# A macaron encoder layer on one Trainium2 core: other pacing of the normalised chunks, norm vectors split once, squares in two buffer tags, half of the last norm's mean added on TensorE

## The chip, the cores and the metric

The kernel runs on one core of one Trainium2 chip. The metric is the device time of one execution in microseconds (us); the number compared is the median of several runs. Engines are named as in the profile: PE is TensorE (matmuls), PEld its weight loads, DVE is VectorE, ACT is ScalarE, POOL is GpSimd, and SP is the queue from which most DMAs are issued.

## The reference

One encoder layer of width 2048 on 256 tokens with 16 learned meta tokens put in front (272 columns in all):

```python
h = LN(ALPHA*h + 0.5*SwiGLU_1(h))                 # norm n1
u = h @ W_in                                      # latents, mLSTM input, output gate
y = [RMSNorm(MLA(u_mla)) | mLSTM_bidir(u_mlstm)] @ W_out
h = LN(ALPHA*h + y)                               # norm n2
h = LN(ALPHA*h + 0.5*SwiGLU_2(h))                 # norm n3
return h[:, 16:]                                  # meta tokens dropped
# SwiGLU(x) = (silu(x @ w_gate) * (x @ w_up)) @ w_down, hidden width 5632
# LN(x) = (x - mean) * rsqrt(var + 1e-5) * g + b
```

All arrays are float32.

## The kernel before

Activations lie transposed, as 16 chunks `z[0..15]` of 128 features by 272 (later 256) tokens; two chunks share one tile `zs[i]`. Every matrix product is made in split precision: a float32 operand is written as a rounded part (hi) and the rest (lo), and `mm3` (L219) sums hi·hi, hi·lo and lo·hi. `mm2` (L225) makes the first two in one matmul of 512 columns.

**Weights.** All weights stream through one line of units of 128 x 1024 (class `Weights`, L78). `_next` (L118) is called when PE's program reaches a new unit. It loads up to four units ahead and splits two units ahead (`_ahead`, L98): ACT casts hi (L113), DVE subtracts to get lo (L114). hi and lo have three buffers each, so a split can start only when PE has left the unit three before. After that `_next` pops at most one entry of `later`, a list of side work that is thus spread at one entry per unit. The whole plan uses 624 units; the constant `UNITS` is 640, so near the end up to four unused units are loaded and two split.

**The order on the engines.** The kernel's program is a straight list. A planner orders each engine's queue from it ahead of time: among the instructions that it reckons ready, the one that stands earliest in the program goes first, so side work that is ready early can move ahead. Once built, each queue is fixed and runs in order.

**Norms.** `Norm` (L263) gathers a layer norm while its chunks are produced. Once chunk number `at` is there, `shift` (L292) subtracts an estimate of the mean; from then on each chunk goes through `sums` (L308): ACT squares it (L305, tile tag `sq`, two buffers), POOL adds chunk and square to running sums (L318, L319), and `scale` (L322) makes chunk times gain in split form for the early product described next. In `scale` ACT multiplies (L328), POOL copies two columns of the gain and bias vectors to the end of the tile (L330), ACT casts (L216) and DVE subtracts (L217).

**The reader of a norm.** `norm_into` (L424) starts the next product before the norm is known: four PSUM tiles (`qt` after n1, `ft` after n2) are made from chunk times gain, and the mean and the scale are put in afterwards by `settle` (L401). At its chunk 4, `rows` (L379) makes the row vectors, and the 16 normalised chunks (`chunk`, L388) become due: ACT makes the bias row (L392), DVE multiplies and adds (L393, L394), ACT casts (L396), POOL subtracts (L398). They are queued on `later` in eight entries (1, 3, ..., 15), and each entry makes two chunks. The next product reads them: four tiles `xm` of 272 columns after n1 (L580), four tiles of feed-forward 2 after n2 (`ffn_up`, L456). Either uses one unit of weights for two chunks, eight units in all. Between the early product and this reader stand the four `settle` steps of the query latents (L543) or the two bodies of `late` (L1048, each two `settle`, a SiLU on ACT, a product and a split).

**The tail.** After the last matmul of feed-forward 2, `moments` (L359) makes the sums of n3. The variance goes through POOL's power (L376), and PE spreads the result over the partitions (`spread`, L249, L258). Meanwhile DVE adds the mean row to all eight pairs `zs` (L1074). Then DVE multiplies each pair by the spread scale (L1078), ACT (six pairs) or POOL (two) apply gain and bias (L1084, L1082), and SP sends each pair out (L1085).

Of the kernel before, what the change touches and what calls it, by code (L numbers as in the profile page):

```python
# [10 lines left out]
F32 = mybir.dt.float32  # L11
F32R = mybir.dt.float32r
AF = mybir.ActivationFunctionType
ALU = mybir.AluOpType
AX = mybir.AxisListType

P = 128
DM = 2048
SEQ = 256
NM = 16  # L20
L = SEQ + NM
# [10 lines left out]
NCD = DM // P  # L32
# [5 lines left out]
ROPE_BASE = 10000.0  # L38
SCALE = (128 + ROPE) ** -0.5
UNIT = 1024  # L40
UNITS = 640
NQ = 4
O_KV = QL
O_KR = QL + KVL
# [33 lines left out]
class Weights:  # L78
# [19 lines left out]
    def _ahead(self):  # L98
        nc = self.nc
        while self.loaded < min(UNITS, self.unit + self.LOADS + 1):  # L100
            u = self.loaded
# [56 lines left out]
def layer(ctx: ExitStack, tc: tile.TileContext, wsrc, xsrc, vsrc, bsrc, csrc, out):  # L158
    nc = tc.nc
    cp = ctx.enter_context(tc.tile_pool(name="cp", bufs=1))  # L160
# [29 lines left out]
    vec = cp.tile([P, NVEC], F32, tag="vec", name="vec")  # L190
    ident = cp.tile([P, P], F32, tag="ident", name="ident")
# [57 lines left out]
    def spread(nm, r, n):  # L249


        def product():
            pr = psum(f"{nm}pr")
            for j, b in enumerate(token_blocks(n)):
                if b % P:
                    nc.tensor.matmul(pr[:, SEQ:L], r[:, j : j + 1].to_broadcast([P, P]), ident[:, P - NM :], start=True, stop=True)
                else:
                    nc.tensor.transpose(pr[:, b : b + P], r[:, j : j + 1].to_broadcast([P, P]), ident)  # L258
            return pr

        return product

    class Norm:  # L263
# [37 lines left out]
                ws.later.append(lambda i=i: (nc.vector.tensor_tensor(self.z[i], self.z[i], cb, ALU.subtract), self.sums(i)))  # L301

        def square(self, c):
            q = sp.tile([P, L], F32, tag="sq", name=f"{self.nm}q{c}")[:, : self.n]
            nc.scalar.activation(q, self.z[c], AF.Square)  # L305
            return q

# [14 lines left out]
        def scale(self, c):  # L322

            g = col(f"{self.ln}_g", c)
            if not self.early:
                return
            s = scratch(f"{self.nm}e{c}")
            nc.scalar.mul(s[:, :SEQ], self.z[c][:, :SEQ], g)  # L328
            o = VEC[f"{self.ln}_g"][0] + 2 * c
            nc.gpsimd.tensor_copy(s[:, SEQ : SEQ + 2], vec[:, o : o + 2])  # L330
            self.e[c] = big(f"{self.nm}e{c}p")
            split(self.e[c], s[:, : SEQ + 2])

        def last(self):
            self.q = self.square(NCD - 1)
# [43 lines left out]
        def rows(self):  # L379

            nm, n = self.nm, self.n
            pr = self.product()
            self.r = sp.tile([P, L], F32, tag="s1", name=f"{nm}r", bufs=1)[:, :n]
            self.nmr = sp.tile([P, L], F32, tag="s2", name=f"{nm}nmr", bufs=1)[:, :n]
            nc.scalar.copy(self.r, pr[:, :n])
            nc.vector.tensor_tensor(self.nmr, self.mb, pr[:, :n], ALU.mult)
# [37 lines left out]
    def norm_into(norm, tiles):  # L424

        norm.last()
        ws.drain()
        xs = Chunks(norm.chunk)
        at = {
            1: norm.moments,  # L430
            2: lambda: norm.scale(NCD - 1),
            4: lambda: (norm.rows(), [ws.later.append(lambda k=k: xs[k]) for k in range(1, NCD, 2)]),
        }
        outer(tiles, Chunks(lambda k: norm.e[k]), SEQ + 2, at)
        return xs
# [17 lines left out]

        return [(psum(f"{nm}{w[0]}{f}"), f"{nm}_w_{w}", [(f * P, P)]) for f in fs for w in ("gate", "up")]

    def ffn_up(nm, x, n, f0, first, hid):  # L456
        f = f0
        while f < NFT:
            fs = list(range(f, f + (first if f == f0 else 1)))
            f = fs[-1] + 1  # L460
            tiles = ffn_tiles(nm, fs)
            wide = n == SEQ
            if len(fs) > 1:
                outer(tiles, x, n, wide=wide)
            else:
                for t in tiles:
                    outer([t], x, n, wide=wide)
            for j, i in enumerate(fs):
                hid.append(hidden(nm, i, n, tiles[2 * j][0], tiles[2 * j + 1][0], wide))
        return hid  # L470
# [14 lines left out]
    x = Chunks(first)  # L485
    norm = Norm("n1", "ln1", L, z, 2.0 * ALPHA, 4.0 * LN_EPS, True)
    hid = ffn_up("ffn1", x, L, 0, 3, [])
    x = None
    ffn_down("ffn1", hid, L, norm)
    hid = None  # L490
# [4 lines left out]
    x = norm_into(nmx, qt)  # L495
    xt = [(psum(f"xm{i}"), "w_in", [(O_XM + i * P, P)]) for i in range(8)]

    class Latent:
# [19 lines left out]
            self.product = rsqrt(self.nm, self.sum, self.n, self.width)  # L518

        def finish(self):  # L520
            pr = self.product()
            for i in range(self.nt):
                u = self.u[i]
                nc.vector.scalar_tensor_tensor(u, u, col(self.gain, i), pr[:, : self.n], ALU.mult, ALU.mult)
                t = big(f"{self.nm}n{i}")
                split(t, u)
                self.out.append(t)
# [12 lines left out]

    uq = Latent("q", 4, SEQ, "mla_q_norm_g", QL)
    ukv = Latent("kv", 2, L, "mla_kv_norm_g", KVL)
    for i in range(4):  # L543
        t, b = nmx.settle(i, qt[i][0])
        nc.scalar.activation(uq.u[i], t, AF.Identity, bias=b)
        uq.add(i)
# [30 lines left out]
        split(t, s)  # L577
        xc.append(t)

    outer(xt[:4], x, L)  # L580
    for i in range(4):
        conv_in(i)
        ws.later.append(lambda i=i: conv_taps(i))
# [35 lines left out]
    for i in range(2):  # L619
        ps = psum(f"ukv{i}")  # L620
# [3 lines left out]
    ps = psum("kr")  # L624
# [56 lines left out]
    e = cp.tile([P, 3, 2, 4], F32, tag="se", name="se")  # L681
# [206 lines left out]
    x = None  # L888
# [102 lines left out]
    norm = Norm("n2", "ln2", SEQ, z, ALPHA, LN_EPS, True, 6)  # L991
# [10 lines left out]
        norm.product = rsqrt("ao", osum[:, :SEQ], SEQ, DA)  # L1002

    def scale_ya():
        pr = norm.product()
        for h in range(NH):
            o = os_[h // 2][:, h % 2, :SEQ]
            nc.vector.scalar_tensor_tensor(o, o, col("attn_out_g", h), pr[:, :SEQ], ALU.mult, ALU.mult)
            ya[h] = big(f"ya{h}")
            split(ya[h], o)  # L1010
# [20 lines left out]
    p, m = pairs[0], ms[0]  # L1031
    for step in (p.keys, p.values, p.rope_rows, p.queries, m.project_q, m.project_k, m.project_v, p.rotate, p.rope_parts, m.scores):
        step()
    for r in range(XH):
        s = steps(r)
# [11 lines left out]
    x = norm_into(nmx, ft)  # L1047
    hid = []  # L1048

    def late(i):  # L1050
        g, gb = nmx.settle(2 * i, ft[2 * i][0])
        u, ub = nmx.settle(2 * i + 1, ft[2 * i + 1][0])
        nc.scalar.activation(g, g, AF.Silu, bias=gb)
        nc.vector.scalar_tensor_tensor(g, u, ub, g, ALU.add, ALU.mult)
        h = big(f"ffn2h{i}")
        split(h, g)
        hid.append(h)

    for i in range(2):
        late(i)  # L1060
    norm = Norm("n3", "ln3", SEQ, z, 2.0 * ALPHA, 4.0 * LN_EPS, False)
    hid = ffn_up("ffn2", x, SEQ, 2, 2, hid)
    x = None
    ffn_down("ffn2", hid, SEQ, norm)
    norm.last()
# [3 lines left out]
    def both(t):  # L1069
        return t[:, :SEQ].unsqueeze(1).to_broadcast(twice)  # L1070

    with tc.issue_after(norm.var.ins):
        for t in zs:
            nc.vector.tensor_tensor(t[:, :, :SEQ], t[:, :, :SEQ], both(norm.mb), ALU.add)  # L1074
    pr = norm.product()
    for i, t in enumerate(zs):
        o = big(f"o{i}", F32)
        nc.vector.tensor_tensor(t[:, :, :SEQ], t[:, :, :SEQ], both(pr), ALU.mult)  # L1078
        for j in range(2):
            c = 2 * i + j  # L1080
            if i in (1, 3):
                nc.gpsimd.tensor_scalar(o[:, j, :SEQ], t[:, j, :SEQ], col("ln3_g", c), col("ln3_b", c), ALU.mult, ALU.add)  # L1082
            else:
                nc.scalar.activation(o[:, j, :SEQ], t[:, j, :SEQ], AF.Identity, bias=col("ln3_b", c), scale=col("ln3_g", c))  # L1084
        nc.sync.dma_start(out[2 * i : 2 * i + 2].rearrange("c p s -> p c s"), o[:, :, :SEQ])  # L1085
# [65 lines left out]
```

## Time and profile before

| | |
|---|---|
| median of 3 runs | 1933.19 us (1931.78 to 1933.21) |
| the profiled execution's own time | 1933.64 us |
| its span in the trace | 1931.8 us |
| PE busy | 1899.5 us (98%) |
| DVE busy | 1109.1 us (57%) |
| ACT busy | 916.5 us (47%) |
| POOL busy | 222.6 us (12%) |
| DMA moved | 336.86 MB, 174 GB/s |
| granted TensorE clock, mean | 0.995 |

The span runs from the first to the last instruction of the program; 1.8 us of the execution lie around it. PE is busy nearly throughout, so time can be saved where PE waits, where it runs at the lower clock, before its first and after its last matmul. Idle time of the other engines costs nothing by itself.

### The profile page before, as it was taken

Reading aid. Unit: us, or ns where it says so; the run is one execution under the profiler, and the core shown is the slowest. Engines: PE = TensorE matmul, PEld = TensorE weight load, DVE = VectorE, ACT = ScalarE, POOL = GpSimd, SP = SyncE. Lnnn points to the kernel's source line nnn. Section 1 sums busy time; section 2 is a strip of 40 time slices with the busy share of each in tenths; the row PEclk is TensorE's granted clock in tenths of the full one; section 3 lists DMA queues with packets and bytes.
Section 4 is the critical chain, followed back from the end, with each engine's and each line's share of the span. In section 5 each row is a group of like instructions: output and inputs, shape, how many; then the busy total and the mean of one; then the engine's idle time right before and its main releaser. Section 6 shows DMA issues by size and latency. Waiting matters only on the chain.

```text
span 1931.8 us, 32349 instructions
## 1 busy us (share of the span) xinstructions
PE 1899.5 (98%) x13089; PEld 1776.7 (92%) x13089; DVE 1109.1 (57%) x1533; ACT 916.5 (47%) x1400; POOL 222.6 (12%) x259
## 2 busy tenths in 40 slices
PE   9999999999999999999999999999999999999996
PEld 9999999999999999989899888888888888888886
DVE  5444444444445544598487788655555555546454
ACT  5333333333333544466576466544444444434433
POOL 0000000000000411231024174000000000003111
PEclk9999999999999999999999999999999999999998
DMA  7444545554554555445422444555555555555554
GB/s 257 179 175 175 175 175 175 175 175 175 175 175 165 184 175 175 164 153 192 164 99 77 140 166 146 200 189 185 188 191 188 185 188 190 189 186 186 190 191 142
DMA packets 97061, 336.86 MB, mean 174 GB/s; under 512 B 10704, under 2 KB 16336, under 8 KB 96912
## 3 DMA queue, kind: packets, MB, share of 16 engines
q1 hardware_dynamic: 96672, 333.97, 49.5%
q8 instruction: 102, 1.67, 0.3%
q0 software_dynamic: 240, 0.84, 0.1%
q14 instruction: 47, 0.39, 0.1%
HBM read 332.67 MB, written 2.10 MB: 173 GB/s over the span
## 4 chain that ended last, share of the span: by engine, by line
PE 93%; DVE 4%; ACT 1%; POOL 1%; issue 1%; DMA 0%; DVEq 0%; ACTq 0%; SPq 0%; POOLq 0%
PE ffn2d L227 8%; PE ffn2u L227 8%; PE ffn2g L227 8%; PE ffn1g L221 5%; PE ffn1u L221 5%; PE ffn1g L223 5%; PE ffn1u L223 5%; PE ffn1g L222 5%; PE ffn1u L222 5%; PE ffn1d L223 4%; PE ffn1d L221 4%; PE ffn1d L222 4%; PE ffn2d L228 4%; PE ffn2g L228 4%; PE ffn2u L228 4%; PE wo L227 2%
## 5 line engine op out<-in xcount | busy, mean ns | idle before, releaser
L114 DVE TENSOR_TENSOR wlo<-raw,whi 128x1024 fp32r<-128x1024 f32 (+2 forms) x634 | 780.8, 1233 | 728.7 <-ACT whi L113 727.1
L113 ACT CAST whi<-raw 128x1024 fp32r<-128x1024 f32 (+2 forms) x634 | 656.6, 1037 | 844.7 <-issue 257.5
L227 PE MATMUL ffn2g<-n2x,whi 128*128 128x512 f32 x672 | 238.4, 394 | 0.0
L227 PE MATMUL ffn2u<-n2x,whi 128*128 128x512 f32 x672 | 238.4, 394 | 0.0
L227 PE MATMUL ffn2d<-ffn2h,whi 128*128 128x512 f32 x660 | 231.2, 394 | 0.0
L221 PE MATMUL ffn1g<-x,whi 128*128 128x272 f32 x704 | 204.0, 290 | 4.7 <-ACT whi L113 4.7
L223 PE MATMUL ffn1g<-x,wlo 128*128 128x272 f32 x704 | 203.9, 290 | 0.0
L223 PE MATMUL ffn1u<-x,wlo 128*128 128x272 f32 x704 | 203.7, 289 | 0.0
L221 PE MATMUL ffn1u<-x,whi 128*128 128x272 f32 x704 | 203.7, 289 | 0.0
L223 PE MATMUL ffn1d<-ffn1h,wlo 128*128 128x272 f32 x704 | 203.4, 289 | 0.2 <-DVE wlo L114 0.2
L222 PE MATMUL ffn1g<-x,whi 128*128 128x272 f32 x704 | 203.5, 289 | 0.0
L221 PE MATMUL ffn1d<-ffn1h,whi 128*128 128x272 f32 x704 | 203.5, 289 | 0.0
L222 PE MATMUL ffn1u<-x,whi 128*128 128x272 f32 x704 | 203.3, 289 | 0.0
L222 PE MATMUL ffn1d<-ffn1h,whi 128*128 128x272 f32 x704 | 202.9, 288 | 0.0
L228 PE MATMUL ffn2g<-n2x,wlo 128*128 128x256 f32 x672 | 189.4, 282 | 4.3 <-DVE wlo L114 4.3
L228 PE MATMUL ffn2u<-n2x,wlo 128*128 128x256 f32 x672 | 188.8, 281 | 0.0
L228 PE MATMUL ffn2d<-ffn2h,wlo 128*128 128x256 f32 x660 | 185.7, 281 | 0.0
L227 PEld LDWEIGHTS ffn2g<-n2x,whi 128*128 128x128 f32 x672 | 126.1, 188 | 29.4
L227 PEld LDWEIGHTS ffn2u<-n2x,whi 128*128 128x128 f32 x672 | 126.2, 188 | 29.2
L227 PEld LDWEIGHTS ffn2d<-ffn2h,whi 128*128 128x128 f32 x660 | 123.8, 188 | 28.5
L221 PEld LDWEIGHTS ffn1g<-x,whi 128*128 128x128 f32 x704 | 132.9, 189 | 4.7 <-ACT whi L113 4.7
L222 PEld LDWEIGHTS ffn1g<-x,whi 128*128 128x128 f32 x704 | 134.4, 191 | 0.0
(1355 smaller groups left out, 3535.5 us busy)
## 6 DMA issues: line engine op xcount, KB each, us to landing
raw<-in_w_dram SPq DMA_DIRECT2D x624, 512.0 KB, 3.2
z<-in_x_dram SPq DMA_DIRECT2D x16, 136.0 KB, 5.3
out_dram<-o SPq DMA_DIRECT2D x8, 256.0 KB, 2.4
raw<-in_w_dram SPq DMA_DIRECT2D x8, 128.0 KB, 3.1
raw<-in_w_dram SPq DMA_DIRECT2D x4, 256.0 KB, 4.7
mask<-in_mask_dram POOLq DMA_DIRECT2D x2, 272.0 KB, 3.2
rope<-in_rope_dram POOLq DMA_DIRECT2D x1, 272.0 KB, 4.8
tri<-in_tri_dram SPq DMA_DIRECT2D x1, 128.0 KB, 3.0
```

Source lines behind the costliest of these rows:

```text
L113: nc.scalar.copy(hi[:, c], self.raw[u][:, c])
L114: nc.vector.tensor_tensor(lo[:, c], self.raw[u][:, c], hi[:, c].bitcast(F32), ALU.subtract)
L221: nc.tensor.matmul(ps, a[0], b[0], start=first, stop=False)
L222: nc.tensor.matmul(ps, a[0], b[1], start=False, stop=False)
L223: nc.tensor.matmul(ps, a[1], b[0], start=False, stop=last)
L227: nc.tensor.matmul(ps, a[0], b[:, :, :SEQ], start=first, stop=False)
L228: nc.tensor.matmul(ps[:, :SEQ], a[1], b[:, 0, :SEQ], start=False, stop=last)
```

## The change

- `UNITS` becomes 624.
- The vectors of the norms are split into hi and lo once (`gb`), when the constants arrive.
- `scale` writes ACT's product straight into the hi part, DVE makes lo as z*g - hi in one instruction, and ACT copies the two columns of `gb`. POOL's copy and ACT's cast go.
- Squares of odd chunks go to tiles of the tag `cv` (two buffers, otherwise the convolution's).
- `norm_into` queues the chunks in 12 entries (0, 1, 2, 3, 4, 6, 7, 9, 10, 12, 13, 15) in place of eight.
- The four query steps and the two `late` bodies move from before the reader's loop into it: queries after its chunks 1, 3, 5 and 7, `late` after chunks 1 and 5.
- In the tail DVE adds the mean to pairs 0 to 3 alone. For pairs 4 to 7 PE makes the sum in PSUM, as two matmuls against the identity; pair 4 stands in front of the spread, pairs 5 to 7 behind it. ACT copies the spread scale to SBUF, and DVE multiplies the four PSUM pairs by that copy.

```diff
-UNITS = 640
+UNITS = 624
...
+    gb = cp.tile([P, 2, 64], F32R, tag="gb", name="gb")
...
         nc.gpsimd.memset(half, -0.5)
+        split(gb, vec[:, :64])
...
         def square(self, c):
-            q = sp.tile([P, L], F32, tag="sq", name=f"{self.nm}q{c}")[:, : self.n]
+            if c % 2:
+                q = sp.tile([P, L + 4], F32, tag="cv", name=f"{self.nm}q{c}")[:, : self.n]
+            else:
+                q = sp.tile([P, L], F32, tag="sq", name=f"{self.nm}q{c}")[:, : self.n]
             nc.scalar.activation(q, self.z[c], AF.Square)
...
-            s = scratch(f"{self.nm}e{c}")
-            nc.scalar.mul(s[:, :SEQ], self.z[c][:, :SEQ], g)
             o = VEC[f"{self.ln}_g"][0] + 2 * c
-            nc.gpsimd.tensor_copy(s[:, SEQ : SEQ + 2], vec[:, o : o + 2])
             self.e[c] = big(f"{self.nm}e{c}p")
-            split(self.e[c], s[:, : SEQ + 2])
+            zc, hi, lo = self.z[c][:, :SEQ], self.e[c][:, 0, :SEQ], self.e[c][:, 1, :SEQ]
+            nc.scalar.mul(hi, zc, g)
+            nc.vector.scalar_tensor_tensor(lo, zc, g, hi.bitcast(F32), ALU.mult, ALU.subtract)
+            nc.scalar.copy(self.e[c][:, :, SEQ : SEQ + 2], gb[:, :, o : o + 2].bitcast(F32))
...
-            4: lambda: (norm.rows(), [ws.later.append(lambda k=k: xs[k]) for k in range(1, NCD, 2)]),
+            4: lambda: (norm.rows(), [ws.later.append(lambda k=k: xs[k]) for k in (0, 1, 2, 3, 4, 6, 7, 9, 10, 12, 13, 15)]),
...
-    for i in range(4):
+
+    def query(i):
         t, b = nmx.settle(i, qt[i][0])
...
-    outer(xt[:4], x, L)
+    outer(xt[:4], x, L, {2 * i + 1: lambda i=i: query(i) for i in range(4)})
...
-    for i in range(2):
-        late(i)
     norm = Norm("n3", "ln3", SEQ, z, 2.0 * ALPHA, 4.0 * LN_EPS, False)
-    hid = ffn_up("ffn2", x, SEQ, 2, 2, hid)
+    hid = ffn_up("ffn2", x, SEQ, 2, 2, hid, {1: lambda: late(0), 5: lambda: late(1)})
...
+    halves = NCD // 4
     with tc.issue_after(norm.var.ins):
-        for t in zs:
+        for t in zs[:halves]:
             nc.vector.tensor_tensor(t[:, :, :SEQ], t[:, :, :SEQ], both(norm.mb), ALU.add)
-    pr = norm.product()
+    centred = [t[:, :, :SEQ] for t in zs[:halves]]
+
+    def centre(i):
+        ps = psum(f"zc{i}").rearrange("p (c s) -> p c s", c=2)
+        nc.tensor.matmul(ps, ident, zs[i][:, :, :SEQ], start=True, stop=False)
+        nc.tensor.matmul(ps, ident, both(norm.mb), start=False, stop=True)
+        centred.append(ps)
+
+    centre(halves)
+    pr, made = norm.product()
+    rs = sp.tile([P, L], F32, tag="s1", name="n3r", bufs=1)
+    nc.scalar.copy(rs[:, :SEQ], pr[:, :SEQ])
+    with tc.issue_after(made.ins):
+        for i in range(halves + 1, NCD // 2):
+            centre(i)
     for i, t in enumerate(zs):
         o = big(f"o{i}", F32)
-        nc.vector.tensor_tensor(t[:, :, :SEQ], t[:, :, :SEQ], both(pr), ALU.mult)
+        nc.vector.tensor_tensor(t[:, :, :SEQ], centred[i], both(pr if i < halves else rs), ALU.mult)
```

`product` (L252) returns its last matmul beside the tile, and `ffn_up` passes `at` on to `outer`; nothing else changes.

## Rows read from the trace of the kernel before

**Rows 1.** The page: busy time of each engine, share of the span, instructions.
```profile
PE 1899.5 (98%) x13089; PEld 1776.7 (92%) x13089; DVE 1109.1 (57%) x1533; ACT 916.5 (47%) x1400; POOL 222.6 (12%) x259
```

**Rows 2.** Who waited for whom, whole span: four of PE's (us, times, longest).
```profile
PE ffn2g L228 <- DVE wlo L114: 4.3, 5, 1.8
PE xm L223 <- DVE wlo L114: 3.6, 5, 1.4
PE wo L228 <- DVE wlo L114: 1.3, 2, 0.8
PE wo L227 <- ACT whi L113: 1.2, 2, 0.9
```

**Rows 3.** Windows: length, PE, PEld, DVE, ACT, POOL busy (instructions), clock, DMA, GB/s.
```profile
829.00:850.00 21.00, 17.29 (x128) 15.97 (x126) 21.00 (x31) 14.95 (x28) 13.10 (x12) 1.00 0.36 126
850.00:856.00 6.00, 6.00 (x48) 6.00 (x49) 3.92 (x3) 1.69 (x3) 0.48 (x1) 1.00 0.72 236
...
1189.00:1210.00 21.00, 16.66 (x88) 13.10 (x88) 20.90 (x35) 14.85 (x25) 9.88 (x9) 1.00 0.36 125
1210.00:1216.00 6.00, 6.00 (x36) 5.26 (x35) 3.35 (x4) 2.10 (x2) 0.00 (x0) 1.00 0.87 276
```

**Rows 4.** Windows around the second half of `wo`, with `scale` and `sums` of n2.
```profile
1125.00:1140.00 15.00, 12.83 (x62) 10.45 (x61) 11.86 (x15) 9.70 (x20) 14.19 (x19) 0.89 0.44 149
1140.00:1165.00 25.00, 25.00 (x147) 22.06 (x146) 19.99 (x27) 15.95 (x25) 13.33 (x15) 1.00 0.57 196
...
1136.00:1140.00 4.00, 4.00 (x16) 3.43 (x15) 3.48 (x5) 2.65 (x6) 3.39 (x6) 0.57 0.64 225
```

**Rows 5.** ACT, then PE, in order of time in the same stretch (start, length).
```profile
1132.14 0.42 ACT L305 ACTIVATE n2q<-z 128x256 f32<-128x256 f32 x1 [2.44 <-POOL n2s L319]
...
1129.85 0.39 PE L228 MATMUL wo<-ya,wlo 128*128 128x256 f32 x1 [0.54 <-DVE wlo L114]
1133.55 0.50 PE L227 MATMUL wo<-ym,whi 128*128 128x512 f32 x1 [0.87 <-ACT whi L113]
1134.81 0.39 PE L228 MATMUL wo<-ym,wlo 128*128 128x256 f32 x1 [0.76 <-DVE wlo L114]
```

**Rows 6.** Groups by line and form, 1109 to 1140 us (busy us, mean ns).
```profile
L330 POOL COPY n2e<-vec 128x2 f32<-128x2 f32 x10 | 5.1, 515 | 0.0
```

**Rows 7.** DVE's groups by line and form, 805 to 853 us.
```profile
L114 DVE TENSOR_TENSOR wlo<-raw,whi 128x1024 fp32r<-128x1024 f32 x14 | 21.2, 1524 | 2.7 <-ACT whi L113 2.7
L394 DVE SCALAR_TENSOR_TENSOR z<-z,vec,n1t 128x272 f32<-128x272 f32 x16 | 10.4, 686 | 0.0
L393 DVE TENSOR_TENSOR z<-z,n1r 128x272 f32<-128x272 f32 x16 | 9.4, 610 | 0.0
```

**Rows 8.** DVE in order of time around the `xm` reader.
```profile
814.03 1.14 DVE L393 TENSOR_TENSOR z<-z,n1r 128x272 f32<-128x272 f32 x3
...
848.06 4.64 DVE L114 TENSOR_TENSOR wlo<-raw,whi 128x1024 fp32r<-128x1024 f32 x3
```

**Rows 9.** All engines in order of time, the tail.
```profile
1911.50 1.23 DVE L114 TENSOR_TENSOR wlo<-raw,whi 128x1024 fp32r<-128x1024 f32 x1 [1.12 <-ACT whi L113]
1913.91 0.42 DVE L288 TENSOR_TENSOR z<-z,ffn2d 128x256 f32<-128x256 f32 x1 [1.19 <-PE ffn2d L223]
...
1916.38 4.91 DVE L1074 TENSOR_TENSOR z<-z,n3mb 128x512 f32<-128x512 f32 x8
1917.71 0.69 PE L258 MATMUL n3pr<-ident,n3st 128*128 128x128 f32 x2 [1.83 <-POOL n3st L376]
1921.20 4.87 DVE L1078 TENSOR_TENSOR z<-z,n3pr 128x512 f32<-128x512 f32 x8
1921.92 6.43 ACT L1084 ACTIVATE o<-z,vec 128x256 f32<-128x256 f32 x12 [5.96 <-DVE z L1078]
```

**Rows 10.** The tail's chain (one float32 product of 256 columns), then two windows.
```profile
1915.00 0.54 PE n3pm L350 x2
...
1919.00:1922.00 3.00, 0.00 (x0) 0.00 (x0) 3.00 (x6) 0.08 (x1) 0.00 (x0) 0.50 0.00 0
```

More of the change, by code (lines that the diff above doesn't have):

```diff
@@ L255, in product @@
                 if b % P:
-                    nc.tensor.matmul(pr[:, SEQ:L], r[:, j : j + 1].to_broadcast([P, P]), ident[:, P - NM :], start=True, stop=True)
+                    made = nc.tensor.matmul(pr[:, SEQ:L], r[:, j : j + 1].to_broadcast([P, P]), ident[:, P - NM :], start=True, stop=True)
                 else:
-                    nc.tensor.transpose(pr[:, b : b + P], r[:, j : j + 1].to_broadcast([P, P]), ident)
-            return pr
+                    made = nc.tensor.transpose(pr[:, b : b + P], r[:, j : j + 1].to_broadcast([P, P]), ident)
+            return pr, made
         return product
@@ L381, in rows @@
             nm, n = self.nm, self.n
-            pr = self.product()
+            pr, _ = self.product()
             self.r = sp.tile([P, L], F32, tag="s1", name=f"{nm}r", bufs=1)[:, :n]
@@ L454, in ffn_tiles, with ffn_up @@
         return [(psum(f"{nm}{w[0]}{f}"), f"{nm}_w_{w}", [(f * P, P)]) for f in fs for w in ("gate", "up")]
-    def ffn_up(nm, x, n, f0, first, hid):
+    def ffn_up(nm, x, n, f0, first, hid, at=None):
         f = f0
@@ L463, in ffn_up @@
             if len(fs) > 1:
-                outer(tiles, x, n, wide=wide)
+                outer(tiles, x, n, at, wide)
             else:
@@ L520, in finish @@
         def finish(self):
-            pr = self.product()
+            pr, _ = self.product()
             for i in range(self.nt):
@@ L1004, in scale_ya @@
     def scale_ya():
-        pr = norm.product()
+        pr, _ = norm.product()
         for h in range(NH):
@@ L1070, in both @@
         return t[:, :SEQ].unsqueeze(1).to_broadcast(twice)
+    halves = NCD // 4
     with tc.issue_after(norm.var.ins):
-        for t in zs:
+        for t in zs[:halves]:
             nc.vector.tensor_tensor(t[:, :, :SEQ], t[:, :, :SEQ], both(norm.mb), ALU.add)
-    pr = norm.product()
+    centred = [t[:, :, :SEQ] for t in zs[:halves]]
[11 more added lines that the diff above has]
+            centre(i)
     for i, t in enumerate(zs):
         o = big(f"o{i}", F32)
-        nc.vector.tensor_tensor(t[:, :, :SEQ], t[:, :, :SEQ], both(pr), ALU.mult)
+        nc.vector.tensor_tensor(t[:, :, :SEQ], centred[i], both(pr if i < halves else rs), ALU.mult)
         for j in range(2):
```

## The prediction

> **What bounds the kernel now.** I read the page first. PE is busy for 98% of the span [rows 1]: weights stream through it, and a change that leaves the matmuls alone can only win where PE waits, runs at the lower clock, or has finished. The table of waits shows the places: PE waited 3.6 us for weight splits in `xm` and 4.3 us in the first tiles of feed-forward 2, and 2.5 us in `wo` [rows 2]. Beside them stands the tail after the last matmul.
>
> At both readers the windows tell more. From 829 to 850 us DVE was busy for all 21 us, while PE got 128 matmuls done; right after, 48 took 6 us, so 128 are worth 16 us, and 5 us were lost. From 1189 to 1210 DVE was busy for 20.9 of 21 us and PE for 16.7: 4.3 us lost, or 6 by count [rows 3]. So DVE bounds the two reader stretches. In `wo` POOL does: it was busy for 14.2 of 15 us from 1125 to 1140. At the pace of the next 25 us (147 matmuls) 62 matmuls are worth 10.5 us, so 4.5 us were lost there, part of it because the clock fell to 0.57 after PE had stood still [rows 4].
>
> **The readers.** A chunk costs DVE a multiply and an add: (10.4 + 9.4) / 16 = 1.24 us, and a split 1.5 us [rows 7]. Both include time in which POOL's own work holds DVE up. From 814.0 to the split that ended PE's last wait (849.8) DVE worked without a pause on all 16 chunks, four queries and nine splits [rows 8]. In the old order all 16 chunks stand before that split, which belongs to the readers' sixth unit. In the new order only chunks 0 to 9 do, as its place is ahead of the entry for chunk 10. Six chunks fewer are 6 x 1.24 = 7.4 us, more than the 5 us lost: the splits would come in time. Feed-forward 2 has the same entries; there 7.4 us stand against 4.3 to 6 us.
>
> What is late next is the chunks. A unit here is 24 matmuls, 3.0 us [rows 3]. Without its waits PE would have started `xm` at about 829.0 and would want chunk 15 in the second half of the eighth unit, at 829.0 + 7 x 3.0 + 1.5 = 851.5. DVE's work up to chunk 15 is that same 35.8 us plus the splits now ahead of it, one to three: it ends between 851.3 and 854.3, and ACT's cast (I put it at DVE's 0.42 for such a width [rows 9]) and POOL's subtraction (13.1 / 12 = 1.1 us [rows 3]) follow. So PE stands for 1.3 to 4.3 us in place of 5.0. I take 3.0 left, a gain of 2.0, and the same 2.0 for feed-forward 2. Bounds: all 5.0 and 6 gone, or, if every instruction ran strictly in program order, more waiting than now (second rival).
>
> The moved steps cost nothing by themselves: a query is still a copy, a multiply and an add on DVE, two activations on ACT and an add on POOL; a `late` body still twice the settling, a SiLU, a product and a split, with no DMA. Behind them on DVE stand the splits two units ahead, counted above. They also free PSUM tiles: four early tiles and four of the reader fill the eight banks, but the next tile is wanted only after the reader's eighth unit, so nobody waits.
>
> **`wo` and the early scaling.** ACT's square stood 2.44 us waiting for POOL to free a square buffer; the weight split queued behind it came late, and PE stood 0.87 and 0.76 us, after which the clock fell [rows 5]. With four square buffers this wait goes, and POOL loses ten copies (5.1 us in this stretch [rows 6]). Of the 4.5 us lost I leave the first wait (0.54 us, about 1.0 with its restart), since there DVE itself was late: gain 3.5. Bounds: nothing, if DVE is late at the other two also, and 4.5. The new add-with-scale on DVE is dearer than the subtraction it replaces, by the gap of about 0.08 us between the two groups [rows 7]: 32 x 0.08 = 2.5 us of DVE beside PE, covered wherever DVE is not full, as it is not from 1140 to 1165 [rows 4]; uncovered in `wo` it costs ten times 0.08, 0.8 us. ACT's cast goes, and a copy of 2 x 2 columns comes, which no row shows: between nothing and a full-width 0.4 us; I take no change. Around n1's shift the same edits are worth at most 0.6 us; I take 0.2.
>
> **Edits at nothing.** The four unused loads and two unused splits ran beside PE's last tile, and DVE stood idle 1.19 us before the last add [rows 9]; if that cover were short they would cost up to that. Splitting the vectors once is one cast and one subtraction of 64 columns, at the time when the constants land; ACT is 47% busy [rows 1]. Uncovered it costs below 1 us.
>
> **The tail.** DVE's eight adds took 4.91 us, 0.61 each, from 1916.38; the spread scale was there at 1917.71 + 0.69 = 1918.40, and the first multiply started only at 1921.20 [rows 9]. With four adds DVE is free at 1916.38 + 4 x 0.61 = 1918.82, 0.4 us after the scale: the first multiply moves by 2.4 us. From there ACT sets the end: twelve activations in 6.43 us, starting 0.72 us after the first multiply [rows 9]. New start 1919.5, new end 1926.0.
>
> PE's sums must keep up. A float32 product of 256 columns took 0.54 us [rows 10], so two of 512 take 1.7 to 2.2 us; I take 1.8. Pair 4 fits into the 1.83 us in which PE waited for POOL's power [rows 9]. Pairs 5, 6 and 7 follow the spread and end near 1920.1, 1921.9 and 1923.7. DVE reaches pair 7 at 1918.8 + 7 x 0.61 = 1923.1, and ACT needs it two activations before its end, at 1924.9. So the last sum has about 0.6 us in hand after DVE's multiply. A multiply of a PSUM pair by an SBUF row is shown nowhere; with the operands the other way round it takes 0.61, and so do the adds from SBUF alone [rows 9], so I take that. ACT's copy of the scale falls into its 5.96 us of idleness. Gain 2.4; bounds 2.6 and a loss of 1.7 (fourth rival).
>
> **The sum.** 2.0 + 2.0 + 3.5 + 0.2 + 2.4 = 10.1 us. Against the profiled execution's own 1933.64 (span 1931.8 and 1.8 around it) this gives 1923.5; that execution lies 0.45 us above the median shown, so against the median I forecast 1923.1 us. About 0.2%, 3.9 us, is what a measurement of this kernel can tell from no change.
>
> **Rivals.**
> - *The readers' waits only change their name.* DVE's queue is full either way [rows 3]; three multiplies ran ahead of the first add, so the planner already departs from the program's order [rows 8], and it may pull the chunks forward again. PE then loses the same 5.0 and 4.3, partly on chunks: 1927.1. Against it stand the six chunks that lose their place. The Trainium skill (SBUF — State Buffer, Who interferes with whom) says that a VectorE instruction with two SBUF inputs and a GpSimd instruction that reads SBUF shut each other out; by that rule pacing spreads such collisions and removes none, which speaks for this rival, and the trace agrees: a split took 1.23 us in the tail [rows 9] and 1.52 in the mean among POOL's subtractions [rows 7]. Chance 0.20.
> - *Slower: the chunks come after their readers.* If DVE and POOL finish chunks 10 to 15 over 2 us after PE wants them, PE stands at the first matmul of each pair. Going through the queue strictly in program order with 1.3 us a chunk, I get 7.1 us of standing in `xm` and 8.3 in feed-forward 2, so 9.1 us more than forecast: 1932.2. After two shorter stands the clock fell in `wo`, where 4 us at 0.57 did 16 matmuls in place of 23.5, 1.3 us lost [rows 4]; with three or four such falls the time is 1936 to 1937. For it: 3 us is all a unit lasts, and chunk 14 is queued only one unit ahead of its reader. Against it: chunks are ready work, which the planner pulls ahead whenever DVE is idle. Chance 0.05.
> - *`wo` keeps its waits*, because DVE, not the square's buffer, holds up the splits there (it was busy for 11.9 of 15 us [rows 4]): 1926.6. Chance 0.10.
> - *PE's sums run at the lower clock.* The clock stood at 0.50 in the tail [rows 10]. At that level a sum takes 3.5 us, pair 7 ends near 1929, and ACT's end moves to 1930.1, 4.1 us later: 1927.2. Against it: PE is now at work where it stood idle before. The Trainium skill (TensorE: Matmul & The Clock Gate, What's actually happening) calls the throttled state the default, which activity releases; by it this hangs on whether the sums follow the last product closely. Chance 0.08.
>
> **The numbers.** The forecast as it stands has 0.55, the rivals 0.43; 0.02 is left for what I don't see. The range reaches down to 1917.5 (a reader's wait wholly gone at both places, 2 + 2.3 us more, and 1 us more in `wo`) and up to 1929.5 (the first rival with half of the `wo` gain missing). Faster by over 0.2% are the forecast and the first, third and fourth rivals, less their combinations: 0.87. Within 0.2%: 0.09. Slower: 0.04, the second rival's upper part.
>
> **What would show it.** In the table of waits: `xm` and `ffn2g` on splits gone, and waits of these two on POOL's L398 below 3 us each. In `wo`: no square waiting for POOL, the clock at 1.00 throughout 1125 to 1140. In the tail: four L1074, the first L1078 right behind the fourth, clock 1.00 during the sums, and ACT's twelve activations without a gap. I would be wrong if PE's lost time at the readers stayed at 5 us each, or if ACT stood between the pairs.

## The result and the profile after

The changed kernel takes 1923.35 us (median of four runs, 1920.99 to 1924.21) against 1933.20 before: ratio 0.9948, interval 0.9935 to 0.9960. The forecast was 1923.1. The profiled execution is the shortest of the four, 1920.99 with a span of 1919.2, so 1.8 us lie around the span again.

The page's engine line and chain after (busy us, share, instructions; answers to [rows 1]):
```profile
PE 1900.7 (99%) x13105; PEld 1776.3 (93%) x13105; DVE 1111.5 (58%) x1528; ACT 906.4 (47%) x1400; POOL 215.9 (11%) x227
...
PE 94%; DVE 4%; issue 1%; ACT 0%; SPq 0%; DMA 0%; POOL 0%; ACTq 0%; DVEq 0%
```
PE is as busy as before and issues 16 matmuls more, the tail's sums (the two of each pair are recorded as two halves). These sums hold it for some 7.5 us, so in the rest of the span it is busy for some 6 us less: what went is time in which it stood, and also time in which it ran slower. The table of waits after (us, times, longest; answers to [rows 2]):
```profile
PE wo L230 <- DVE wlo L114: 3.5, 3, 1.3
PE ffn2g L229 <- POOL n2x L403: 1.6, 2, 1.3
PE xm L225 <- DVE wlo L114: 1.5, 5, 0.4
...
PE wo L229 <- ACT whi L113: 0.4, 1, 0.4
```
`xm` waits 1.5 us in place of 3.6 and still for splits; `ffn2g` 1.6 in place of 4.3, and now for chunks. **`wo` waits longer than before**: 3.5 + 0.4 against 1.3 + 1.2.

A wait lasts from an engine's stop to its restart, and lost pace around it isn't in it. So the comparison below goes by places in the work: the start of the first or the last matmul of a tile name. The view of one tile gives them, here for before, then after (count, ns min/median/max, first and last start):
```profile
L221 PE MATMUL xm<-n1x,whi x128: 284/288/373, 829.4 to 883.2; 128*128 128x272 f32 x128
L223 PE MATMUL xm<-n1x,wlo x128: 283/289/394, 830.8 to 883.4; 128*128 128x272 f32 x128
...
L227 PE MATMUL wo<-ym,whi x128: 388/393/628, 1057.5 to 1161.0; 128*128 128x512 f32 x128
...
L221 PE MATMUL ffn2g<-n2e0p,whi x2: 281/282/282, 1164.2 to 1164.9; 128*128 128x258 f32 x2
...
L227 PE MATMUL ffn2d<-ffn2h,whi x660: 390/393/586, 1665.4 to 1896.4; 128*128 128x512 f32 x165
...
L223 PE MATMUL ffn2d<-ffn2h,wlo x44: 276/281/291, 1897.0 to 1913.6; 128*128 128x256 f32 x44
```
```profile
L223 PE MATMUL xm<-n1x,whi x128: 284/288/372, 827.6 to 879.0; 128*128 128x272 f32 x128
L225 PE MATMUL xm<-n1x,wlo x128: 283/288/397, 828.4 to 879.2; 128*128 128x272 f32 x128
...
L229 PE MATMUL wo<-ym,whi x128: 389/393/582, 1051.6 to 1155.1; 128*128 128x512 f32 x128
...
L223 PE MATMUL ffn2g<-n2e0p,whi x2: 282/282/283, 1158.2 to 1159.0; 128*128 128x258 f32 x2
...
L229 PE MATMUL ffn2d<-ffn2h,whi x660: 390/393/587, 1655.7 to 1886.3; 128*128 128x512 f32 x165
...
L225 PE MATMUL ffn2d<-ffn2h,wlo x44: 275/280/290, 1886.9 to 1903.5; 128*128 128x256 f32 x44
```
The stretches between such starts, in us, of the profiled execution of every kernel in this study (E1 to E11 are the experiments; `wo` runs from its first matmul to the first of `ffn2g`, the tail from the last matmul of `ffn2d` to the span's end):

| kernel | first matmul | to `uq` | to `xm` | `xm` | to `wo` | `wo` | `ffn2g`, `ffn2u` | `ffn2d` | tail | span |
|---|---|---|---|---|---|---|---|---|---|---|
| before | 4.7 | 798.8 | 25.9 | 54.0 | 174.1 | 106.7 | 501.2 | 248.2 | 18.2 | 1931.8 |
| after | 4.1 | 798.1 | 25.4 | 51.6 | 172.4 | 106.6 | 497.5 | 247.8 | 15.7 | 1919.2 |
| E1 eight entries | 4.0 | 798.8 | 25.9 | 53.2 | 174.2 | 106.7 | 499.0 | 247.9 | 15.7 | 1925.4 |
| E2 side work first | 4.2 | 798.4 | 25.5 | 51.7 | 174.1 | 106.7 | 498.9 | 248.2 | 15.7 | 1923.4 |
| E3 old `scale` | 4.0 | 798.5 | 25.4 | 51.6 | 174.0 | 107.4 | 495.8 | 248.1 | 15.6 | 1920.4 |
| E4 two squares | 4.1 | 798.5 | 25.4 | 51.6 | 172.3 | 107.3 | 497.5 | 247.8 | 15.7 | 1920.2 |
| E5 old tail | 4.0 | 798.8 | 25.4 | 51.6 | 173.9 | 106.6 | 497.5 | 247.9 | 18.0 | 1923.7 |
| E6 640 units | 4.3 | 798.9 | 25.4 | 51.6 | 174.0 | 106.6 | 497.4 | 247.9 | 15.8 | 1921.9 |
| E7 `scale` later | 4.6 | 797.9 | 25.4 | 51.6 | 173.9 | 106.1 | 498.4 | 248.1 | 15.7 | 1921.7 |
| E8 chunk's lo on DVE | 4.5 | 798.3 | 25.4 | 48.7 | 172.4 | 106.6 | 497.2 | 247.9 | 15.7 | 1916.7 |
| E9 E7 + six squares | 4.1 | 798.4 | 25.4 | 51.6 | 174.0 | 103.6 | 497.4 | 248.1 | 15.7 | 1918.3 |
| E10 all of these | 4.1 | 798.9 | 25.5 | 48.7 | 173.8 | 103.7 | 495.2 | 248.1 | 15.8 | 1913.8 |
| E11 three pairs on DVE | 4.1 | 798.5 | 25.4 | 51.6 | 172.4 | 106.6 | 498.5 | 247.8 | 16.7 | 1921.6 |

From before to after the span lost 12.6 us: 2.4 in `xm` and 0.5 ahead of it, **3.7 in `ffn2g` with `ffn2u`, 0.1 in `wo`**, 2.5 in the tail, 0.4 in `ffn2d`, 1.3 before `uq`, and 1.7 between `xm` and `wo`, where the change touches nothing. That last stretch takes 172.3 to 172.4 or 173.8 to 174.2 in all thirteen kernels, with nothing between. The long form has a fall of the granted clock (last section), which the profiled execution of after happened not to have. The start of `uq` scatters too: it lies at 802.2 to 803.2 us in after and the seven experiments that leave untouched what stands ahead of it, and at 803.5 in before. Without these two stretches (1.7 and 1.3 us) the parts sum to 9.6 us, and the medians differ by 9.85. The same kind of scatter is in `ffn2g` with `ffn2u`: E11, whose edit lies in the tail, takes 498.5 us there against 497.5, with a wait of 0.8 us on a split that after doesn't have. So in that column about 1 us can't be put down to an edit by the stretch alone. `wo` is steadier: 106.6 to 106.7 us in all kernels that have the change's own form there.

In `wo`, PE's waits after, then DVE around the first two, in order of time (start, length):
```profile
1124.66 0.39 PE L230 MATMUL wo<-ya,wlo 128*128 128x256 f32 x1 [1.07 <-DVE wlo L114]
1128.90 0.39 PE L230 MATMUL wo<-ym,wlo 128*128 128x256 f32 x1 [1.19 <-DVE wlo L114]
1133.22 0.39 PE L230 MATMUL wo<-ya,wlo 128*128 128x256 f32 x1 [1.26 <-DVE wlo L114]
...
1120.40 0.95 DVE L336 SCALAR_TENSOR_TENSOR n2e3p<-z,vec,n2e3p 128x256 fp32r<-128x256 f32 x1
1121.27 0.96 DVE L336 SCALAR_TENSOR_TENSOR n2e4p<-z,vec,n2e4p 128x256 fp32r<-128x256 f32 x1
1122.16 0.75 DVE L303 TENSOR_TENSOR z<-z,n2cb 128x256 f32<-128x256 f32 x2
1122.83 1.77 DVE L114 TENSOR_TENSOR wlo<-raw,whi 128x1024 fp32r<-128x1024 f32 x1
1124.52 0.95 DVE L336 SCALAR_TENSOR_TENSOR n2e5p<-z,vec,n2e5p 128x256 fp32r<-128x256 f32 x1
...
1127.06 1.79 DVE L114 TENSOR_TENSOR wlo<-raw,whi 128x1024 fp32r<-128x1024 f32 x1
1128.77 0.95 DVE L336 SCALAR_TENSOR_TENSOR n2e7p<-z,vec,n2e7p 128x256 fp32r<-128x256 f32 x1
```
and the same stretch by windows (length, PE, PEld, DVE, ACT, POOL, clock, DMA, GB/s; answers to [rows 4]):
```profile
1105.00:1145.00 40.00, 36.49 (x205) 31.04 (x204) 39.80 (x54) 23.85 (x52) 28.41 (x26) 1.00 0.50 161
```
No square stands behind POOL's sums any more, but DVE is busy for 39.8 of 40 us, and PE starts 0.05 to 0.06 us after each late split ends. ACT had the hi parts of the three late units ready 2.3, 1.5 and 2.4 us before DVE began their splits (casts from 1119.51, 1124.49 and 1127.96, of 1.03 to 1.05 us), so the splits stood in DVE's queue. They take 1.77 us, against 1.23 in the old tail [rows 9].

DVE is full there mainly because the change itself fills it. The same 40 us, counted from the start of `wo`, first in before, then in E3, which has the old `scale`:
```profile
1111.00:1151.00 40.00, 37.83 (x205) 32.41 (x204) 35.40 (x53) 26.16 (x51) 30.67 (x37) 0.96 0.44 154
...
1107.00:1147.00 40.00, 37.42 (x201) 31.70 (x200) 35.87 (x53) 26.20 (x51) 30.64 (x37) 0.96 0.47 154
```
Over n2's 16 chunks the old subtraction took 0.72 us in the mean in before (0.42 to 0.97) and 0.70 in E3. The add-with-scale takes 0.94: 0.62 once and 0.95 to 0.97 fifteen times. That is 0.22 us dearer each, 3.5 us in all.

The tail after, all engines in order of time (answers to [rows 9]):
```profile
1903.65 1.02 PE L1085 MATMUL zc<-z,ident 128*128 128x512 f32 x2
...
1906.40 2.50 DVE L1080 TENSOR_TENSOR z<-z,n3mb 128x512 f32<-128x512 f32 x4
...
1907.99 1.02 PE L1085 MATMUL zc<-z,ident 128*128 128x512 f32 x2
...
1908.81 2.48 DVE L1098 TENSOR_TENSOR z<-z,n3pr 128x512 f32<-128x512 f32 x4
...
1909.53 6.43 ACT L1104 ACTIVATE o<-z,vec 128x256 f32<-128x256 f32 x12 [0.91 <-DVE z L1098]
1909.71 1.02 PE L1085 MATMUL zc<-z,ident 128*128 128x512 f32 x2
...
1911.20 1.89 DVE L1098 TENSOR_TENSOR z<-zc,n3r 128x512 f32<-128x512 f32 x3
...
1913.42 0.69 DVE L1098 TENSOR_TENSOR z<-zc,n3r 128x512 f32<-128x512 f32 x1 [0.33 <-PE zc L1086]
```
The first multiply stands 2.41 us behind the first add, where it stood 4.82 before. PE's sums follow each other at 1.72 us (1907.99, 1909.71), DVE waits 0.33 us for the last, and ACT's twelve activations run in 6.43 us as before.

### The profile page after: what moved, and what is told of

Its sections match the earlier page's. It is cut to its first block, busy times and chain, and to the rows that moved or that the text cites. A ratio compares the mean times of both kernels' runs of the same rounds, so it can differ in the third digit from the quotient of the medians.

```text
span 1919.2 us, 32307 instructions
## 1 busy us (share of the span) xinstructions
PE 1900.7 (99%) x13105; PEld 1776.3 (93%) x13105; DVE 1111.5 (58%) x1528; ACT 906.4 (47%) x1400; POOL 215.9 (11%) x227
## 4 chain that ended last, share of the span: by engine, by line
PE 94%; DVE 4%; issue 1%; ACT 0%; SPq 0%; DMA 0%; POOL 0%; ACTq 0%; DVEq 0%
PE ffn2d L229 8%; PE ffn2g L229 8%; PE ffn2u L229 8%; PE ffn1d L223 5%; PE ffn1d L225 5%; PE ffn1d L224 5%; PE ffn1g L225 5%; PE ffn1u L223 5%; PE ffn1u L225 5%; PE ffn1g L223 5%; PE ffn1u L224 5%; PE ffn1g L224 5%; PE ffn2d L230 4%; PE ffn2g L230 4%; PE ffn2u L230 4%; PE wo L229 2%
```

## The experiments

All edits are made to the changed kernel; 1923.35 us is what to compare with. Ratios are to the kernel before, with their intervals; its median, taken anew beside each group of experiments, was 1932.5 to 1933.2 us, so differences below 1 us between groups say little.

**E1, the old eight entries.**
```diff
-(0, 1, 2, 3, 4, 6, 7, 9, 10, 12, 13, 15)
+range(1, NCD, 2)
```


> The changed kernel with the old eight entries of two chunks each; the query and late steps stay inside the readers' loops. If the pacing of the chunks is what freed DVE for the splits, the splits come late again: PE loses some 5 us in xm and 4 to 5 us in ffn2g (changed kernel: 2.7 and 2.0 by the gaps between matmuls), and the time is about 1928. If the planner pulls the chunks forward whatever the entries say, and the moved query and late steps made the gain, both readers lose what they lose now and the time stays within 1 us of 1923.4.


Measured: 1925.78 us (1925.53 to 1927.19), 0.9970 [0.9958, 0.9981]. Two lines of its table of waits:
```profile
PE xm L225 <- DVE wlo L114: 3.1, 5, 1.0
PE ffn2g L230 <- DVE wlo L114: 2.6, 3, 1.8
```
The waits on splits come back at both readers, and `xm` takes 53.2 us, `ffn2g` with `ffn2u` 499.0. So pacing is worth 1.6 of the 2.4 us gained in `xm`, the whole 0.5 ahead of it, and 1.5 of the 3.7 in feed-forward 2 (about 1 us of that column is scatter). The time came out between the two that were expected, 1928 and 1923.4.

**E2, queries and `late` ahead of the readers again, twelve entries kept.**
```diff
-    outer(xt[:4], x, L, {2 * i + 1: lambda i=i: query(i) for i in range(4)})
+    for i in range(4):
+        query(i)
+    outer(xt[:4], x, L)
...
+    for i in range(2):
+        late(i)
-    hid = ffn_up("ffn2", x, SEQ, 2, 2, hid, {1: lambda: late(0), 5: lambda: late(1)})
+    hid = ffn_up("ffn2", x, SEQ, 2, 2, hid)
```


> The changed kernel with the four query steps and the two late bodies again ahead of the readers' loops; the twelve entries stay. If the pacing makes the gain, the splits of the readers' first units come late by part of the 3.8 us (queries) and 5.3 us (late) that stand ahead of them: 1 to 2 us lost more at each reader, time 1925 to 1927. If the moved steps make the gain, both readers lose about 5 us again and the time is about 1928.


Measured: 1925.30 us (1924.93 to 1926.42), 0.9965 [0.9952, 0.9978]. Two lines of its table of waits:
```profile
PE ffn2g L229 <- POOL n2x L403: 3.0, 3, 2.3
PE xm L224 <- POOL n1x L403: 2.2, 2, 1.3
```
With side work ahead of the chunks, the chunks are late, as the second rival has it, though for less. In feed-forward 2 the move of `late` is worth 1.4 us (498.9 against 497.5). In `xm` the move of the queries is worth 0.1: the wait changes its name, and the stretch stays at 51.7. With E1 this leaves 0.7 us of the gain in `xm` and 0.8 in feed-forward 2 that neither edit alone gives back; no run has both undone.

**E3, the old `scale`; E4, all squares in the tag `sq`.**
```diff
-            nc.scalar.mul(hi, zc, g)
-            nc.vector.scalar_tensor_tensor(lo, zc, g, hi.bitcast(F32), ALU.mult, ALU.subtract)
-            nc.scalar.copy(self.e[c][:, :, SEQ : SEQ + 2], gb[:, :, o : o + 2].bitcast(F32))
+            nc.scalar.mul(s[:, :SEQ], self.z[c][:, :SEQ], g)
+            nc.gpsimd.tensor_copy(s[:, SEQ : SEQ + 2], vec[:, o : o + 2])
+            split(self.e[c], s[:, : SEQ + 2])
```


> The changed kernel with the old scale: ACT's product and cast, POOL's copy of two columns, DVE's subtraction. If DVE's queue as a whole bounds wo from 1108 to 1135, the subtraction is no cheaper there than the add-with-scale (both stretched by POOL to 0.96 us) and wo loses 4 to 5 us as now, time within 1 us of 1923.4. If the add-with-scale is the dearer one (0.96 against the 0.42 of an undisturbed subtraction), wo loses 1 to 2 us and the time is 2 to 3 us lower.


```diff
-            if c % 2:
-                q = sp.tile([P, L + 4], F32, tag="cv", name=f"{self.nm}q{c}")[:, : self.n]
-            else:
-                q = sp.tile([P, L], F32, tag="sq", name=f"{self.nm}q{c}")[:, : self.n]
+            q = sp.tile([P, L], F32, tag="sq", name=f"{self.nm}q{c}")[:, : self.n]
```


> The changed kernel with all squares in the two buffers of the old tag. If ACT's wait for a square buffer costs PE something beside DVE's lateness, it is back with 2 us or more, the cast queued behind it comes late, and wo loses 6 to 7 us: time about 1926. If DVE's lateness alone sets wo, ACT may wait but PE loses 4 to 5 us there as now, time within 1 us of 1923.4.


Measured: E3 1922.03 us (1921.66 to 1922.49), 0.9947 [0.9930, 0.9964]; E4 1923.58 us (1921.97 to 1925.88), 0.9956 [0.9941, 0.9971]. Neither form's time can be told from the change's own. In `wo` each old form alone costs 0.7 to 0.8 us, for different reasons. In E3 DVE has room again and PE waits less than in after (2.0 us on splits and 0.9 on casts, against 3.5 and 0.4), but ACT stands up to 2.9 us behind POOL's copies, and the clock falls to 0.50 from 1135.1 to 1138.5. In E4 squares stand for POOL again (1.8 and 1.5 us), PE waits as long as in after (3.2 and 0.8), and the clock stays at 1.00. E3 gets its loss back, and 0.9 us more, in feed-forward 2; why stays open.

**E5, the old tail; E6, 640 units.** E5 puts back the eight adds and multiplies on DVE without PE's sums and ACT's copy.


> The changed kernel with the old tail: eight mean additions on DVE, none on PE. If four of DVE's additions were all that stood between the spread scale and the first multiply, the time from the last feed-forward matmul to the end of the span is 18.2 us again in place of 15.7, and the time is 2.4 to 2.6 us above the changed kernel's, about 1925.9. If the end is set by the outgoing transfers, the tail stays below 16.5 us and the time within 1 us of 1923.4.


```diff
-UNITS = 624
+UNITS = 640
```


> The changed kernel with UNITS at 640 again: four unused loads and two unused splits near the end. My theory: covered by PE's last tile, time within 1 us of 1923.4 and tail 15.7 us. Rival: the unused splits or loads delay the last add or the outgoing transfers, tail 16.5 us or more and the time 1 us or more above.


Measured: E5 1924.61 us (1923.35 to 1925.70), 0.9958 [0.9943, 0.9973]; E6 1923.56 us (1923.27 to 1923.88), 0.9953 [0.9938, 0.9967]. E5's tail in order of time:
```profile
1908.45 4.90 DVE L1079 TENSOR_TENSOR z<-z,n3mb 128x512 f32<-128x512 f32 x8
...
1913.28 4.86 DVE L1083 TENSOR_TENSOR z<-z,n3pr 128x512 f32<-128x512 f32 x8
```
The multiply stands 4.83 us behind the first add again, and the tail takes 18.0 us against 15.7. By the trace the new tail is worth 2.3 us; the medians show 1.3, with runs that overlap. In E6 the unused units cost nothing that shows.

**E7, half of n2's scaling put off.** `wo`'s waits had become DVE's. E7 moves the early scaling of chunks 0 to 6 to beside the sums of chunks 8 to 14.
```diff
-            self.scale(c)
+            if self.at == NQ:
+                self.scale(c)
+            elif c > self.at:
+                self.scale(c)
+                if c > 7:
+                    self.scale(c - 8)
```


> The changed kernel, but after n2's shift the early scaling of chunks 0 to 6 (seven products on ACT and seven add-with-scale on DVE) is put off and done beside that of chunks 8 to 14, so that it falls into the later part of wo. If DVE's queue bounds wo between 1108 and 1135, this takes 7 x 0.9 = 6 us off it there, the three splits come in time, and wo loses 1 to 2 us in place of 4.7: time about 1920.5. If the splits are late for another reason (the shift's own subtractions, POOL), wo still loses 4 us or more and the time stays within 1 us of 1923.4.


Measured: 1922.73 us (1922.59 to 1923.49), 0.9949 [0.9934, 0.9964]; `wo` 106.1. In its `wo`, ACT in order of time:
```profile
1121.40 0.42 ACT L310 ACTIVATE n2q<-z 128x256 f32<-128x256 f32 x1 [2.62 <-POOL n2s L324]
```
With DVE relieved, the wait of the old kernel [rows 5] is back, four square buffers or not: PE's waits on splits fall to one of 1.6 us (and 0.7 on casts), the clock falls to 0.50 again (1127.9 to 1131.3), which takes back most of that, and the stretch gains 0.5 us. POOL is the next bound right behind DVE.

**E9, E7 with squares in six buffers.**
```diff
-            if c % 2:
-                q = sp.tile([P, L + 4], F32, tag="cv", name=f"{self.nm}q{c}")[:, : self.n]
-            else:
-                q = sp.tile([P, L], F32, tag="sq", name=f"{self.nm}q{c}")[:, : self.n]
+            q = scratch(f"{self.nm}q{c}")[:, : self.n]
```


> The changed kernel with the early scaling of n2's chunks 0 to 6 put off as in the run before, and all squares in six scratch buffers instead of four. Theory: in wo DVE and POOL bound each other (each reads SBUF through what the other needs), and whichever is relieved, the other's backlog shows: with the scaling put off, ACT stood waiting for POOL to free a square. With both relieved wo loses under 2 us in place of 4.7 (4.0 with the scaling put off alone), time about 1920.5. Rival: the splits come late for a reason outside these two, wo still loses 4 us and the time stays within 1 us of 1922.7.


Measured: 1920.49 us (1918.49 to 1921.08), 0.9935 [0.9920, 0.9950]. In its table of waits one split is left:
```profile
PE wo L230 <- DVE wlo L114: 0.8, 1, 0.8
```
`wo` takes 103.6 us, 3.0 less than after, and the median falls by 2.9. Here are 3.0 of the 3.5 us that the change was forecast to win in `wo`, and they came with both bounds moved. Six buffers without E7's delay were not run; that they would give nothing alone is an argument, from the fact that in after no square stands for POOL.

**E8, the chunk's last subtraction on DVE in place of POOL.**
```diff
-            eng = nc.gpsimd
+            eng = nc.vector
```


> The changed kernel with the subtraction that ends each normalised chunk on DVE in place of POOL. It adds 16 x 0.38 = 6 us to DVE at each reader and takes POOL's work away from beside it. If POOL's reads are what stretches DVE there, DVE's instructions fall back to 0.42 (multiply), 0.49 (add) and 1.22 (split), DVE's total stays about the same, the waits of ffn2g on POOL's chunks go, and the time is 0 to 2 us below the changed kernel's. If DVE is stretched by something else, its load grows by 6 us per reader, PE loses 4 us or more again at each, and the time is 3 to 6 us above.


Measured: 1919.31 us (1918.39 to 1920.24), 0.9931 [0.9915, 0.9948], so 4.0 us below the change. DVE's groups from 807 to 852 us, after first, then E8 (busy us, mean ns; answers to [rows 7]):
```profile
L114 DVE TENSOR_TENSOR wlo<-raw,whi 128x1024 fp32r<-128x1024 f32 x14 | 19.2, 1380 | 3.7 <-ACT whi L113 3.7
L399 DVE SCALAR_TENSOR_TENSOR z<-z,vec,n1t 128x272 f32<-128x272 f32 x16 | 12.2, 783 | 0.0
L398 DVE TENSOR_TENSOR z<-z,n1r 128x272 f32<-128x272 f32 x16 | 7.9, 539 | 0.0
```
```profile
L114 DVE TENSOR_TENSOR wlo<-raw,whi 128x1024 fp32r<-128x1024 f32 x15 | 18.3, 1217 | 3.1 <-ACT whi L113 3.1
L399 DVE SCALAR_TENSOR_TENSOR z<-z,vec,n1t 128x272 f32<-128x272 f32 x16 | 8.1, 524 | 0.0
L403 DVE TENSOR_TENSOR n1x<-z,n1x 128x272 fp32r<-128x272 f32 x16 | 7.1, 466 | 0.0
L398 DVE TENSOR_TENSOR z<-z,n1r 128x272 f32<-128x272 f32 x16 | 6.3, 433 | 0.0
```
DVE does 16 subtractions and one split more for 0.5 us more (39.8 against 39.3 us), since everything else on it gets shorter: 783 to 524 ns, 539 to 433, 1380 to 1217. PE no longer waits in `xm`, which falls to 48.7 us. The Trainium skill (SBUF — State Buffer, Who interferes with whom) has DVE's second pair of ports shared with GpSimd under an exclusive lock; these rows agree in that DVE's instructions get shorter when GpSimd's leave, and give the price of those. That the lock is what stretches them is not shown by them.

**E10, E8 and E9 together, with `late` after chunks 5 and 11.**
```diff
-    hid = ffn_up("ffn2", x, SEQ, 2, 2, hid, {1: lambda: late(0), 5: lambda: late(1)})
+    hid = ffn_up("ffn2", x, SEQ, 2, 2, hid, {5: lambda: late(0), 11: lambda: late(1)})
```


> All of the previous run, with the chunks' last subtraction on DVE, and the late bodies after the reader's chunks 5 and 11 in place of 1 and 5. If the three places are independent, xm loses nothing, ffn2g under 1.5 us (2.2 with the subtraction alone on DVE) and wo under 2 us: time about 1916. If the gains overlap (wo's time reappears at the reader of n2), the time is 1918.5 or more.


Measured: **1915.08 us** (1913.27 to 1915.54), 0.9906 [0.9889, 0.9922], the fastest of the study, 8.3 us below the change. Against after its stretches are 2.9 shorter in `xm`, 2.9 in `wo`, 2.3 in feed-forward 2, 8.1 together. Of the last, E8 alone has 0.3; whether the rest belongs to the later `late` bodies alone was not tried.

**E11, three pairs on DVE and five sums on PE.**
```diff
-    halves = NCD // 4
+    halves = 3
```


> The changed kernel with three of the mean's additions on DVE and five on PE. The first multiply is then bound by the spread scale, 0.4 us earlier. Theory: PE's sums (1.72 us each, four behind the spread) become the bound: the last pair is ready some 1.5 us after DVE wants it, ACT's last two activations wait, and the tail is 16.0 to 16.8 us in place of 15.7. Rival: DVE's additions were still the bound, the tail is 15.3 us.


One run, so that only its trace is used: 1923.35 us. Its tail takes 16.7 us against 15.7, in order of time:
```profile
1910.05 1.88 DVE L1098 TENSOR_TENSOR z<-z,n3pr 128x512 f32<-128x512 f32 x3 [0.36 <-ACT n3r L1092]
...
1914.82 0.69 DVE L1098 TENSOR_TENSOR z<-zc,n3r 128x512 f32<-128x512 f32 x1 [1.03 <-PE zc L1086]
...
1916.53 0.69 DVE L1098 TENSOR_TENSOR z<-zc,n3r 128x512 f32<-128x512 f32 x1 [1.03 <-PE zc L1086]
```
With one pair more PE's sums are the bound: DVE waits 1.03 us for each of the last two. Four and four is the better split.

## Why the prediction was right, and where it was not

The total came out (1923.1 forecast, 1923.35 measured), and that it came out so closely is luck. The term for `wo` was 3.4 us too large; the two readers' terms were 2.6 us too small, and 0.5 us more came in the tail and in `ffn2d`.

- **`wo`, forecast 3.5, measured 0.1.** The step that failed: "ACT's square stood 2.44 us waiting for POOL to free a square buffer; the weight split queued behind it came late". The square's wait did go, and the splits stayed late, because DVE, which I put down as late at the first of three waits only, is late at all of them. PE waits 1.4 us more than before, about what the fall of the clock that went had cost (1.3 us by [rows 4]). That is the third rival's outcome, given 0.10, though its reason is only half of the truth: before, the square's buffer was a bound, and E7 shows it as the bound right behind DVE. The sum had DVE's load wrong in two ways. DVE busy for 11.9 of 15 us beside POOL's 14.2 [rows 4] isn't free time, since DVE's own instructions stretch while POOL works. And the add-with-scale, **forecast 0.08 us dearer each** from groups of other instructions [rows 7], was 0.22 dearer: 3.5 us of DVE over the 16 chunks, where I named 0.8 for ten and left it out of the sum. Relieving DVE alone gave 0.5 us (E7), relieving DVE and POOL's buffers gave 3.0 (E9). E3 and E4 have half of the edit each, and their `wo` takes 107.4 and 107.3 us, longer than with both halves (106.6) or neither (106.7): the parts don't add up. Both signs that I had named for this step came, no square waiting for POOL and a clock of 1.00 throughout; they told of the cause that I had in mind, and not of PE's time.
- **Readers, forecast 2.0 + 2.0, measured 2.4 with 0.5 ahead of it, and 3.7.** The mechanism held, the size was low. I set the new wait on chunks at 3.0 us in each reader; measured are 1.6 in `ffn2g`, and in `xm` no wait on chunks at all but 1.5 on splits, which I had said would come in time. "What is late next is the chunks" holds for feed-forward 2 alone. I also priced the moved steps at nothing: right for the queries (0.1, E2), wrong for the `late` bodies, whose place is worth some 1.4.
- **The tail, forecast 2.4, measured 2.5.** Each step was met: the first multiply 2.4 us earlier, a sum at 1.72 us (1.8 forecast), 0.33 us of waiting for pair 7 (0.6 forecast), ACT without a gap. The multiply of a PSUM pair took 0.63 (1.89 / 3; 0.61 forecast). The fourth rival didn't come: the granted clock stayed at full speed until 1918.7, after the sums. E11 shows how near PE's bound was.
- **Columns copied by ACT, between 0 and 0.4:** 0.18 us. **Units and vectors split once, nothing:** E6 agrees; the vectors' cast and subtraction took 0.25 and 0.22 us at 31.6 and 32.5 us, and PE waited for nothing from 15 to 60 us. **Around n1's shift, forecast 0.2:** too small to be seen in the scatter ahead of `uq`.
- **First rival** (waits change their name only): refuted for the change as a whole, true of the queries' move in `xm`. **Second rival** (chunks late, slower): the waits came in E2 in its form, 2.2 and 3.0 us, a third of its price.
- **The range's ends** don't follow from the terms named for them: 1923.1 - 5.3 is 1917.8, not 1917.5, and half of the `wo` gain on top of 1927.1 is 1928.9, not 1929.5. The measured time lies well inside either way.

## What to carry to other kernels

Before a wait is costed as gone, ask of every engine on that stretch how much room it has, and take an engine as fuller than its busy share when its instructions run longer there than elsewhere: in `wo` the square's buffers and DVE held the splits up by turns, and the 3 us came when both were moved. Price a new instruction by what runs in the stretch where it will stand: the add-with-scale saved ACT a cast and POOL a copy, and put 3.5 us on DVE, which was the engine short of room. Handing work from a full DVE to GpSimd need not be a relief (with the 16 subtractions of `xm` on GpSimd DVE was busy for 0.5 us less, and `xm` took 2.9 us more); compare DVE's mean durations with and without it, as E8 does. Side work that shares a queue with a paced reader should be put where the reader can still spare it: the same two bodies were worth some 1.4 us by their place alone.

## What the runs showed of the hardware that was not expected

- The granted clock fell to 0.50, the level of 1.2 GHz, about 0.6 us after 24 matmuls of 4 columns each (`cum`), though PE was busy throughout. PE in before, in order of time:
```profile
947.44 0.20 PE L705 MATMUL cum<-sf,tri 16*16 16x4 f32 x2
...
948.14 0.52 PE L652 MATMUL pz<-whi,n1x 128*128 128x512 f32 x1
...
948.88 0.63 PE L651 MATMUL pz<-wlo,n1x 128*128 128x512 f32 x1
```
  The fall lasted from 948.3 to 951.7, and products of 512 columns took 0.63 us in it against 0.39 around it. The four kernels whose stretch from `xm` to `wo` takes 172.3 to 172.4 us ran the same matmuls without it. Of three of these four (after, E4, E8) there are other executions: their mean clock is 0.998 to 0.999, against 1.00 in the profiled one. So it seems to come in some executions of one kernel and not in others; it is worth about 1.7 us of the scatter between runs.
- In after, PE stood 1.07, 1.19 and 1.26 us in `wo`, some 4.3 us apart, and the clock stayed at 1.00. Before, it fell behind waits of 0.87 and 0.76, which lay 1.3 us apart [rows 4, 5]. In `wo` of E4 PE stood 0.43 and 1.25 us, 1.8 us apart, without a fall; in E3 0.55 and 1.19 us, 1.7 us apart, with one. The length of a single wait did not decide it.
- POOL's subtractions beside DVE cost DVE as much as doing them itself: a multiply-add on DVE took 783 ns with them and 524 without, a split 1380 and 1217.
